# A routed expert layer in pairs of experts: 64 places each, side by side in column halves, with unsplit float32 weights

## The chip, the cores and the metric

The kernel runs on one core of one Trainium2 chip. The metric is the device time of one execution in microseconds (us), the median of several runs. The profile is one further execution, recorded by the hardware profiler; its own time and its span stand below.

## What is computed

The program is one network for 256 tokens of 1024 channels: a first block (three mixing branches, then a routed layer of experts) and a second block of four attention and feed-forward layers. The change is in the routed layer, cut here to what matters:

```python
def hier_moe(h, lp):                       # t: (256, 1024)
    g_logits = t @ lp["moe_rg_w"] + lp["moe_rg_b"]          # 4 groups
    p_top, g_sel = lax.top_k(jax.nn.softmax(g_logits, axis=-1), 1)
    ...                                     # 4 experts in a group, the best two are taken
    e_top, e_sel = lax.top_k(e_in_group, MOE_TOPK)
    w_sel = p_top * jax.nn.softmax(e_top, axis=-1)
    ...
    hg = jnp.einsum("nd,edh->neh", t, lp["moe_w_gate"])      # 16 experts, 1024 -> 256
    hu = jnp.einsum("nd,edh->neh", t, lp["moe_w_up"])
    a = jax.nn.silu(hg) * hu * combine[..., None]
    return jnp.einsum("neh,ehd->nd", a, lp["moe_w_down"])    # 256 -> 1024
```

Each token uses two experts of one group. The result is multiplied by a modulation row and added to the tokens, and a norm and the second block follow. With the inputs of the reference the four groups get 58, 53, 86 and 59 tokens, and no expert gets more than 53.

## The kernel before

Every dense product is a split product: a float32 weight tile is loaded (`raw`, four buffers), ScalarE casts it to a high part (L240), VectorE subtracts to get the low part (L242), and TensorE runs three float32r matmuls, high by high, high by low and low by high (L254, L255, L256). `Core.unit` is that load with its split, `Core.mm3` the three matmuls.

The routed layer is `Block1.moe` (L1451) with its helpers:

- `logits` (L1269) transposes the tokens and multiplies by the routing weights, while `rms` and L1468, L1469 write the normalised tokens `xp` as high and low parts.
- `route` (L1284) is a chain of small VectorE operations in two steps. The first picks each token's group (`top`, L1301 to L1305). `places` (L1337) turns the group marks into places inside the group, by matmuls with a triangle of ones, and reads the fullest group's count into a register of every engine. The second step picks the two experts and their weights.
- `experts` (L1356) works by groups: 128 places a group. One-hot marks (L1370) gather the tokens by matmuls (L1382) into transposed tiles of two groups, which are split again (L1384 to L1386). For each of the 16 experts it streams gate and up weights in four units, 24 matmuls of 512 columns, then SiLU and the product with the token's weight, two transposes (L1444), and the down product of the expert before, 12 matmuls of 512 columns. After each group the result is split and scattered back to the tokens (L1417).
- `add_experts` (L1496) multiplies by the modulation row and adds to the tokens.
- A second, conditional pass for groups of over 128 tokens stands behind it in a block that is skipped at run time (L1493).

TensorE's order is fixed in part by `issue_after`. The eight steps of `mod_row(5)` (L1207), which computes the modulation row from `ada_w`, are the `filler` between `logits`, `route` and `places`. In `ada_steps` (L671, matmul L684) four float32 matmuls stand side by side in 32-column strips. Weight loads go out on SP's queue, small constants and rows on POOL's.

In the second block `enter` (L2026) multiplies the tokens by the final norm's weights (L2037) and transposes them (L370) for the first projection.

## Time and profile before

| | us |
|---|---|
| median of 3 runs | 2035.04 (2033.83 to 2035.51) |
| the profiled execution, its own time | 2037.31 |
| its span in the trace | 2035.5 |
| TensorE busy (PE) | 1931.8 (95%) |
| VectorE busy (DVE) | 1336.6 (66%) |
| ScalarE busy (ACT) | 1035.3 (51%) |
| DMA, mean over the span | 179 GB/s |

PE, DVE, ACT and POOL are the engines' busy times in the span of the profiled execution, which lies 1.8 us under that execution's own time. All places below are us from the start of that span. `arena` is the one large buffer from which most tiles are cut, `mm` and `acc` are PSUM banks (three and five of them), so instructions are told apart by their line. PEld is the loading of weights into the array, and a queue's name ends in q.

### The profile page before, as it was taken

The page shows a single profiled execution, that of the slowest core. Times are in us where ns is not written, and L with a number is a line of the kernel's source. Part 1 is how long each engine was busy: PE and PEld are TensorE (multiplying, and loading weights), DVE is VectorE, ACT ScalarE, POOL GpSimd, SP SyncE. Part 2 cuts the span into 40 slices and gives each one's busy share as a digit, 9 for nine tenths or more (in the row PEclk, how much of TensorE's full clock was granted, in tenths as well). Part 3 has the DMA queues.
Part 4 walks back from the last instruction along what each step waited for, and adds up shares of the span by engine and source line. Part 5 has one row for each costly group of instructions (what it writes and reads, how often), then busy time and mean ns, then how long its engine had stood idle before and what let it go on. Part 6 is the DMA issues. An engine that isn't in the chain of part 4 may idle for free.

```text
span 2035.5 us, 27804 instructions
## 1 busy us (share of the span) xinstructions
PE 1931.8 (95%) x10012; PEld 1546.8 (76%) x10012; DVE 1336.6 (66%) x2324; ACT 1035.3 (51%) x1656; POOL 135.9 (7%) x259
## 2 busy tenths in 40 slices
PE   6998998989998999999999999999999999999997
PEld 2886886867786678887888877887767888767886
DVE  4689887868897775556555466556566555867555
ACT  5555654546774744434655555443563444454442
POOL 2110000000002000002111200000110000300000
PEclk8999998989998899999999999999999999989999
DMA  9546644777995356654543456664554655435662
GB/s 310 162 140 194 183 139 147 236 247 245 321 323 162 116 166 199 186 176 131 170 136 110 147 178 202 191 186 145 156 176 129 201 187 176 155 104 175 188 189 80
DMA packets 272403, 364.61 MB, mean 179 GB/s; under 512 B 17018, under 2 KB 206677, under 8 KB 272256
## 3 DMA queue, kind: packets, MB, share of 16 engines
q1 hardware_dynamic: 264832, 338.38, 52.5%
q0 software_dynamic: 7424, 24.36, 3.8%
q8 instruction: 81, 1.33, 0.3%
q14 instruction: 66, 0.54, 0.1%
HBM read 359.53 MB, written 3.15 MB: 178 GB/s over the span
## 4 chain that ended last, share of the span: by engine, by line
PE 59%; DVE 6%; ACT 2%; DMA 1%; issue 1%; POOL 0%; SPq 0%; DVEq 0%; ACTq 0%; POOLq 0%
PE mm L254 14%; PE mm L255 13%; PE mm L256 13%; PE acc L254 4%; PE acc L256 4%; PE acc L255 4%; PE acc L1752 1%; PE acc L1650 1%; DVE arena L242 1%; PE acc L1929 1%; PE acc L2117 1%; ACT arena L240 1%; DVE arena L2014 1%; PE acc L1749 1%; DMA arena<-in_w_gate_up 1%; PE acc L1925 1%
## 5 line engine op out<-in xcount | busy, mean ns | idle before, releaser
L242 DVE TENSOR_TENSOR arena<-arena,arena 128x1024 fp32r<-128x1024 f32 x597 | 716.9, 1213 | 480.6 <-ACT arena L240 475.8
L240 ACT CAST arena<-arena 128x1024 fp32r<-128x1024 f32 x597 | 614.0, 1039 | 549.4 <-PE mm L256 298.9
L254 PE MATMUL mm<-arena 128*128 128x512 f32 (+1 forms) x1856 | 703.3, 385 | 12.7 <-ACT arena L240 6.8
L255 PE MATMUL mm<-arena 128*128 128x512 f32 (+1 forms) x1856 | 706.0, 381 | 0.3 <-DVE arena L242 0.3
L256 PE MATMUL mm<-arena 128*128 128x512 f32 (+1 forms) x1856 | 698.7, 380 | 3.5 <-DVE arena L1386 1.3
L254 PEld LDWEIGHTS mm<-arena 128*128 128x128 f32 x1856 | 352.9, 191 | 85.8 <-ACT arena L240 8.3
L256 PEld LDWEIGHTS mm<-arena 128*128 128x128 f32 x1856 | 352.3, 191 | 71.2 <-DVE arena L219 4.1
L255 PEld LDWEIGHTS mm<-arena 128*128 128x128 f32 x1856 | 354.0, 191 | 61.5 <-issue 1.8
L254 PE MATMUL acc<-arena 128*128 128x512 f32 (+5 forms) x736 | 235.5, 360 | 7.3 <-ACT arena L218 7.3
L255 PE MATMUL acc<-arena 128*128 128x512 f32 (+5 forms) x736 | 235.4, 351 | 0.5 <-DVE arena L219 0.5
L256 PE MATMUL acc<-arena 128*128 128x512 f32 (+4 forms) x736 | 231.8, 350 | 0.0
L218 ACT CAST arena<-acc 128x512 fp32r<-128x512 f32 (+2 forms) x174 | 92.7, 542 | 179.1 <-PE acc L2117 79.8
L219 DVE TENSOR_TENSOR arena<-acc,arena 128x512 fp32r<-128x512 f32 (+2 forms) x174 | 108.1, 632 | 99.1 <-ACT arena L218 98.7
L254 PEld LDWEIGHTS acc<-arena 128*128 128x128 f32 (+1 forms) x736 | 125.0, 190 | 40.3 <-issue 11.6
L255 PEld LDWEIGHTS acc<-arena 128*128 128x128 f32 (+1 forms) x736 | 125.7, 190 | 21.6 <-issue 1.8
L256 PEld LDWEIGHTS acc<-arena 128*128 128x128 f32 (+1 forms) x736 | 124.7, 190 | 20.5 <-DVE arena L219 1.7
L1685 ACT ACTIVATE arena<-arena,nm 128x128 f32<-128x128 f32 (+2 forms) x128 | 65.9, 517 | 27.1 <-DVE nm L1684 27.1
L768 DVE SCALAR_TENSOR_TENSOR arena<-arena 128x192 f32<-128x192 f32 (+1 forms) x160 | 64.9, 430 | 2.4 <-ACT arena L766 0.9
L1684 DVE CUSTOM_DVE_ANT_0 arena<-acc,arena 128x128 f32<-128x128 f32 (+2 forms) x128 | 53.1, 465 | 13.6 <-PE acc L256 13.6
L370 PE MATMUL acc<-arena 128*128 128x128 f32 x200 | 32.9, 302 | 24.1 <-DVE arena L1020 8.2
L370 PEld LDWEIGHTS acc<-arena 128*128 128x128 f32 x200 | 24.4, 153 | 34.8 <-DVE arena L1020 8.3
L2101 ACT ACTIVATE arena<-mm 128x256 f32<-128x256 f32 x88 | 32.4, 379 | 24.4 <-PE mm L256 11.9
(354 smaller groups left out, 1497.8 us busy)
## 6 DMA issues: line engine op xcount, KB each, us to landing
arena<-in_w_gate_up SPq DMA_DIRECT2D x352, 256.0 KB, 4.0
arena<-in_w_down SPq DMA_DIRECT2D x88, 512.0 KB, 3.6
arena<-in_b_w_qkv SPq DMA_DIRECT2D x144, 256.0 KB, 3.0
arena<-in_w_in SPq DMA_DIRECT2D x56, 512.0 KB, 4.0
arena<-in_ada_w SPq DMA_DIRECT2D x48, 512.0 KB, 5.7
arena<-in_moe_w_gate SPq DMA_DIRECT2D x64, 256.0 KB, 4.6
arena<-in_moe_w_up SPq DMA_DIRECT2D x64, 256.0 KB, 4.9
arena<-in_moe_w_down SPq DMA_DIRECT2D x32, 512.0 KB, 5.3
```

The costliest lines, as they stand in the source:

```text
L218: self.nc.scalar.copy(h, src)
L219: self.nc.vector.tensor_sub(l, src, h.bitcast(F32))
L240: nc.scalar.copy(h[:, : nk * n], raw[:, : nk * n])
L242: nc.vector.tensor_sub(l[:, : nk * n], raw[:, : nk * n], h[:, : nk * n].bitcast(F32))
L254: yield t.matmul(out, x[0], w[0], start=start, stop=False)
L255: yield t.matmul(out, x[0], w[1], start=False, stop=False)
L256: yield t.matmul(out, x[1], w[0], start=False, stop=stop)
L370: self.nc.tensor.transpose(ps[:, j * P : (j + 1) * P], src[:, j * P : (j + 1) * P], self.ident)
L768: nc.vector.scalar_tensor_tensor(ov[:, rows], x, w, ov[:, rows], ALU.mult, ALU.add)
L1684: nc.vector.tensor_tensor_reduce(pr, s, mask, -0.125, 3e38 if sink is None else sink, ALU.add, ALU.min, nm)
L1685: nc.scalar.activation(pr, pr, AF.Exp, bias=nm, scale=-1.0, accum_out=l)
L2101: nc.scalar.activation(s, ps[:, :256], AF.Silu)
```

## The change

- Experts are taken in eight pairs, with 64 places for each expert. The two experts of a pair write partitions 0 to 63 and 64 to 127 of the same PSUM tile, by matmuls on the two column halves of the array.
- The experts' weights and activations are float32 and unsplit: one float32 matmul where three float32r matmuls stood. Loads are 512 KB each with 4 KB in a row, 12 for a pair. To get such rows a partition takes eight consecutive channels; `xp` is written in that order and the two modulation columns are turned into it through DRAM.
- 9216 words of the float32r arena become nine more float32 weight buffers during the layer ("switched"), so that 13 buffers take the loads in turn.
- `route` finds the experts in its first step, and `places` counts places for each expert. The block for experts of over 64 tokens stands after the transposes of the second pair.
- The tokens themselves are put into the sum by a matmul with the identity, each pair's result is multiplied by the modulation row before it is scattered, and the second block reads the sum from PSUM. `add_experts` falls away.
- `mod_row(5)` runs with the Hyena branch, after `mod_row(2)`.

The core of the diff:

```diff
-LATER = (0, 2, 4, 6)
-MORE = (5, 2)
+MORE, SEATS, YP, AMID = 9, 64, 2, 1
-FILL = (3, 4, 1)
...
+    def close_switched(self):
+
+        a = self.arenas[F32R]
...
+        self.arenas["switched"] = Arena(self.switched_room(F32, "f"), SWITCHED)
...
+        turned = []
+        for i, m in enumerate((self.S2, self.A2)):
+            d = self.dram.tile([D], F32, name=f"mod2{i}")
+            nc.gpsimd.dma_start(d.rearrange("(k p) -> p k", p=P), m.rearrange("p k o -> p (k o)"))
+            turned.append(self.tile((KT, 1), F32, f"mod2{i}", 1, "moe"))
+            nc.gpsimd.dma_start(turned[-1].rearrange("p k o -> p (k o)"), d.rearrange("(p k) -> p k", p=P))
...
+        def gather_two(h, g, k):
+            ps = c.mm().rearrange("p (k s) -> p k s", k=2)
+            for j in range(2):
+                cols = slice((k + j) * P, (k + j + 1) * P)
+                for i in range(4):
+                    mm(ps[:, j], xp[i // 2][i % 2][:, cols], marks(i // 2, 4 * g, 4), start=i == 0, stop=i == 3)
+                nc.scalar.activation(h[:, k + j], ps[:, j], AF.Identity, bias=self.S2e[:, k + j], scale=self.A2e[:, k + j])
...
+        def scatter(p, ohT, y):
+            yp = self.parts((D,), "y", YP, "moe")
+            for n in range(2):
...
+                nc.vector.tensor_tensor(f, y[n], self.rows[5][:, sl], ALU.mult)
+                c.split(*(a[:, sl] for a in yp), f)
+            yield
             for t in range(2):
...
+                        mm(acc[t][n], ohT[:, t], yp[i][:, 512 * n : 512 * n + 512], start=False, stop=first == 0 and p == 7 and i == 1)
...
+        for p in range(8):
...
+            hq = [h[:, :, p % 2 * P + 64 * e : p % 2 * P + 64 * e + 64] for e in range(2)]
+            ps = c.acc()
+            for k in range(0, KT, 4):
+                for i, name in enumerate(("moe_w_gate", "moe_w_up")):
+                    us = [load(I[name][0, 2 * p + e].rearrange("(p k) n -> p k n", p=P)[:, k : k + 4]) for e in range(2)]
+                    for j in range(4):
+                        for e in range(2):
+                          with c.after(order):
+                            mm(ps[64 * e : 64 * e + 64, 256 * i : 256 * i + 256], hq[e][:, k + j], us[e][:, j], start=i + k + j == 0, stop=i + k + j == KT)
...
+            with then():
+                next(late, None)
...
+            if p == AMID and amid is not None:
+                with self.tc.If(amid > SEATS):
+                    for n in range(SEATS, 256, SEATS):
+                        self.experts(xp, acc, n, raw)
+                    mark()
+                    for k in range(0, KT // 2, 2):
+                        gather_two(following, 1, k)
+            with then():
+                following = next(later, None)
+            then()
+            y = [c.mm(), c.mm()]
             for kk in range(2):
+                wd = [load(I["moe_w_down"][0, 2 * p + e, kk * P : (kk + 1) * P].rearrange("p (o n) -> p o n", o=1)) for e in range(2)]
+                for n in range(2):
+                    for e in range(2):
+                      with c.after(order):
+                        mm(y[n][64 * e : 64 * e + 64], aT[:, kk, 64 * e : 64 * e + 64], wd[e][:, 0, 512 * n : 512 * n + 512], start=kk == 0, stop=kk == 1)
+            late = scatter(p, ohT, y)
+            next(late)
+            with then():
+                following = next(later, None)
...
+        acc = [[c.acc() for n in range(2)] for t in range(2)]
+        for t in range(2):
+            for n in range(2):
+                with c.after(c.last(PE)):
+                    nc.tensor.matmul(acc[t][n], c.ident, xs[t][:, 512 * n : 512 * n + 512], start=True, stop=False)
...
-        self.add_experts(self.experts(xp, 0, unit), xs)
-        with self.tc.If(most > P):
-            self.add_experts(self.experts(xp, P, own_unit), xs)
+        rooms = rooms()
+        self.experts(xp, acc, 0, lambda: next(rooms), most)
+        return acc
...
-            weave(self.hyena(), self.merge_branch(2, acc), self.mod_row(2))
+            weave(self.hyena(), self.merge_branch(2, acc), chain(self.mod_row(2), self.mod_row(5)))
...
-            for sl in HALVES:
-                nc.vector.tensor_tensor(zs[t][:, sl], xs[t][:, sl], nf[:, sl], ALU.mult)
+            for sl, ps in zip(HALVES, sums[t]):
+                nc.vector.tensor_tensor(zs[t][:, sl], ps, nf[:, sl], ALU.mult)
```

## Rows read from the trace of the kernel before

**Rows 1.** Busy us of each engine by stage, granted clock, DMA share, GB/s.

```profile
355.00:428.00 73.00, 71.87 (x342) 58.40 (x341) 54.44 (x76) 33.73 (x44) 4.47 (x7) 1.00 0.68 223
428.00:459.00 31.00, 23.72 (x172) 17.82 (x172) 24.74 (x76) 13.74 (x25) 1.65 (x3) 0.72 0.83 278
459.00:617.00 158.00, 151.51 (x680) 121.81 (x679) 134.40 (x147) 115.04 (x147) 0.00 (x0) 0.99 0.87 292
```

**Rows 2.** Timeline of TensorE: two experts' beginnings, and the last expert matmul.

```profile
601.74 0.40 PE L254 MATMUL acc<-arena 128*128 128x512 f32 x1
...
610.55 0.40 PE L254 MATMUL acc<-arena 128*128 128x512 f32 x1
...
616.86 0.39 PE L256 MATMUL mm<-arena 128*128 128x512 f32 x1
```

**Rows 3.** Groups of the expert stage, 458.7 to 617: VectorE's weight split.

```profile
L242 DVE TENSOR_TENSOR arena<-arena,arena 128x1024 fp32r<-128x1024 f32 x92 | 110.4, 1223 | 17.5 <-ACT arena L240 15.3 <-DMA arena<-in_moe_w_up 0.6 <-DMA arena<-in_moe_w_down 0.3
```

**Rows 4.** Timeline of TensorE and VectorE: routing, 428 to 459.

```profile
428.15 1.50 PE L684 MATMUL acc<-arena 128*32 128x256 f32 x24
...
439.77 1.27 DVE L1469 SCALAR_TENSOR_TENSOR arena<-arena,rm,arena 128x1024 fp32r<-128x1024 f32 x1
...
443.26 0.15 DVE L1301 TENSOR_REDUCE r<-arena 128x2 f32<-128x8 f32 x1
...
446.81 0.16 DVE L1304 TENSOR_REDUCE r<-arena 128x2 f32<-128x8 f32 x1
447.00 0.17 DVE L1305 TENSOR_TENSOR arena<-arena,r 128x8 f32<-128x8 f32 x1
...
456.03 0.74 PE L1382 MATMUL mm<-arena 128*128 128x256 f32 x4
...
458.73 0.48 PE L254 MATMUL mm<-arena 128*128 128x512 f32 x1
```

**Rows 5.** Line L684 in PSUM `acc`: records, ns min/median/max, places.

```profile
L684 PE MATMUL acc<-arena x128: 379/379/636, 326.0 to 453.0; 128*32 128x256 f32 x128
```

**Rows 6.** Timeline of TensorE: unsplit float32 in four strips, and on the whole array.

```profile
326.05 1.07 PE L684 MATMUL acc<-arena 128*32 128x256 f32 x16
...
339.88 0.64 PE L684 MATMUL acc<-arena 128*32 128x256 f32 x8
340.44 0.39 PE L254 MATMUL acc<-arena 128*128 128x256 f32 x1
...
346.16 1.02 PE L1219 MATMUL acc<-arena 128*128 128x256 f32 x4
```

**Rows 7.** Line L1493, the skipped block: ns of each engine's branch, and place.

```profile
L1493 PEldq COMPARE_BRANCH  x1: 3599/3599/3599, 618.7 to 618.7; - x1
...
L1493 DVEq COMPARE_BRANCH  x1: 72/72/72, 623.3 to 623.3; - x1
L1493 DVEq EVENT_SEMAPHORE  x1: 21/21/21, 626.4 to 626.4; - x1
```

**Rows 8.** A stretch of mixed expert loads, DMA engines full, columns as rows 1.

```profile
509.30:513.30 4.00, 3.69 (x19) 2.73 (x18) 4.00 (x6) 2.79 (x6) 0.00 (x0) 1.00 1.06 394
```

**Rows 9.** DMA packets in 357.3 to 361.3, then in 573.3 to 577.3.

```profile
DMA packets 760, 1.60 MB, mean 401 GB/s; under 512 B 48, under 2 KB 48, under 8 KB 759
...
DMA packets 1437, 1.39 MB, mean 347 GB/s; under 512 B 82, under 2 KB 1437, under 8 KB 1437
```

**Rows 10.** DMA issues on the page: KB each, us to landing.

```profile
arena<-in_w_down SPq DMA_DIRECT2D x88, 512.0 KB, 3.6
```

**Rows 11.** Waits between 320 and 430: us in total, times, longest.

```profile
POOL arena L1260 <- DVE arena L219: 11.9, 1, 11.9
```

**Rows 12.** Timeline of TensorE: the second block's first transposes.

```profile
627.27 1.97 PE L370 MATMUL acc<-arena 128*128 128x128 f32 x8 [7.68 <-DVE arena L2037]
```

**Rows 13.** Stretches with unsplit float32 alone on TensorE, columns as rows 1.

```profile
28.00:36.00 8.00, 5.65 (x53) 2.45 (x52) 6.34 (x24) 7.32 (x15) 2.19 (x4) 1.00 0.98 329
40.00:48.00 8.00, 7.62 (x32) 3.75 (x36) 3.85 (x8) 6.81 (x10) 1.63 (x3) 0.50 0.84 288
```

More of the change, by code (lines that the diff above doesn't have):

```diff
@@ L1321, in route @@
         m2 = top(eg, h2)
+        both = tile(2, 4)
+        v.tensor_tensor(both, h1, h2, ALU.add)
+        spread = lambda x: x.rearrange("p t (o j) -> p t o j", o=1).to_broadcast([P, 2, 4, 4])
+        v.tensor_tensor(self.marks.rearrange("p t (g j) -> p t g j", g=4), spread(both), by, ALU.mult)
+        yield
+        v.tensor_tensor(ex, g, along(mx), ALU.subtract)
+        nc.scalar.activation(ex, ex, AF.Exp)
         q, d = tile(2), tile(2)
@@ L1354, in places, with experts @@
         return nc.values_load(most_i[0:1, 0:1], min_val=0, max_val=256)
-    def experts(self, xp, first, unit):
+    def experts(self, xp, acc, first, raw, amid=None):
         c, nc, I = self.c, self.nc, self.I
         tile = lambda shape, dt, tag, bufs=1: self.tile(shape, dt, tag, bufs, "moe")
-        parts = lambda shape, tag, bufs=1: self.parts(shape, tag, bufs, "moe")
+        mm = nc.tensor.matmul
         pos = self.pos
         if first:
-            pos = tile((2, 4), F32, "later")
+            pos = tile((2, 16), F32, "later")
@@ new lines, in experts, with then @@
+        late, later = iter(()), iter(())
+        order = c.last(PE)
+        def then():
+            nonlocal order
+            order = c.last(PE)
+            return c.after(order)
+        for p in range(8):
+            if p % 2 == 0 and p:
+                h = following
+            if p % 2 == 0 and p < 6:
+                later = gather(p // 2 + 1)
+            hq = [h[:, :, p % 2 * P + 64 * e : p % 2 * P + 64 * e + 64] for e in range(2)]
[7 more added lines that the diff above has]
+                            mm(ps[64 * e : 64 * e + 64, 256 * i : 256 * i + 256], hq[e][:, k + j], us[e][:, j], start=i + k + j == 0, stop=i + k + j == KT)
+            wp = c.mm()[:, :2]
+            for t in range(2):
+                mm(wp, marks(t, 2 * p, 2).bitcast(F32), self.comb[:, t, 2 * p : 2 * p + 2], start=t == 0, stop=t == 1)
+            for e in range(2):
+                rows = slice(64 * e, 64 * e + 64)
+                nc.scalar.copy(weight[rows, p : p + 1], wp[rows, e : e + 1])
@@ L1445, in experts @@
-            aT = parts((2, P), "aT", 2)
-            c.split(*(x.rearrange("p k t -> p (k t)") for x in aT), ps[:, : 2 * P])
-            pend = (e, aT, y)
-        down(*pend)
-        return acc
-    def moe(self, xs, fill):
-        c, nc = self.c, self.nc
-        def filler(n):
-            for _ in range(n):
-                with c.after(c.last(PE)):
-                    next(fill)
-        filler(FILL[0])
+            nc.vector.scalar_tensor_tensor(a, ps[:, 256:], weight[:, p : p + 1], s, ALU.mult, ALU.mult)
@@ L1460, in moe @@
+            next(late)
+            with then():
+                following = next(later, None)
+            then()
+        next(late)
+    def moe(self, xs):
+        c, nc = self.c, self.nc
+        c.close_switched()
         pss = self.logits(xs)
         first = c.last(DVE), c.last(ACT)
-        filler(FILL[1])
         r = self.rms(xs, [c.norm_f_tile()] * 2)
@@ L1496, in add_experts, with rooms @@
-    def add_experts(self, acc, xs):
-        for t in range(2):
-            for n in range(2):
-                sl = slice(512 * n, 512 * n + 512)
-                a = self.tile((512,), F32, "moa", 2, "moe")
-                self.nc.vector.tensor_tensor(a, acc[t][n], self.rows[5][:, sl], ALU.mult)
-                self.nc.vector.tensor_tensor(xs[t][:, sl], xs[t][:, sl], a, ALU.add)
+        other = lambda: c.arenas["switched"].ring("moe", "wx", 1024, MORE)
+        def rooms():
+            while True:
+                for f, n in ((c.raw, RAW), (other, MORE)):
+                    for _ in range(n):
+                        yield f()
@@ L1571, in run @@
                 self.dump(f"mix{t}", xs[t])
-            self.moe(xs, self.mod_row(5))
-            for t in range(2):
-                self.dump(f"moe{t}", xs[t])
+            sums = self.moe(xs)
             drop("moe", "mrow5")
-        return xs
+        return xs, sums
 def rope_tables(c):
@@ L2163, in network @@
         b1 = Block1(core)
-        xs = b1.run()
+        xs, sums = b1.run()
         core.first_block_done()
-        Block2(core, b1.tables).run(xs, out)
+        Block2(core, b1.tables).run(xs, sums, out)
 def kernel(**inputs):
```

184 lines of the change are left out of this document (83 added, 101 removed).

## The prediction, made before the changed kernel was run

> **What bounds it now.** I read the busy times by stage first. From 459 to 617 the routed experts keep TensorE busy 151.5 of 158 us at a granted clock of 0.99, while VectorE has 134 and the DMA engines a share of 0.87 [rows 1]. So TensorE sets the pace, and the timeline gives it: one expert every 8.81 us, for 36 matmuls of 512 columns and two transposes, or some 0.23 us a matmul [rows 2]. VectorE's weight split, 110 us of 92 subtractions [rows 3], lies beside that. Ahead of it, from 428 to 459, TensorE's clock is 0.72 on average [rows 1] and the path is VectorE's chain of small routing operations, broken by weight splits: the normalised tokens end at 441.04, the next routing operation starts at 443.26, and its fourth only at 446.81, though two dependent ones need 0.19 us each [rows 4]. Behind it the last expert matmul starts at 616.86 [rows 2] and the second block's first transposes at 627.27 [rows 12]: between them lie the scatter, eight VectorE operations and the skipped block, where TensorE's branch alone takes 3.6 us [rows 7].
>
> **Ahead of the experts.** `mod_row(5)` moves to a stage in which TensorE is busy 71.9 of 73 us [rows 1], so its work is paid there. Half of the 128 records of L684 in `acc` are its own: 64 records for 32 matmuls, so an unsplit float32 matmul runs as two passes [rows 5]. In four strips 16 passes take 1.07 us, and full-width passes come every 0.214 us, (1.02 - 0.379)/3 [rows 5, 6]; a change between strips and full width costs 0.13 us, since eight passes, worth 0.43, hold the next matmul up by 0.56 [rows 6]. That makes 16 rounds of 0.215, eight passes of L1219 and some sixteen changes: 3.4 + 1.7 + 1.7 = 6.8 us. I take all of it; the end for a stage that hides half is 3.4. Its four more megabytes of loads lie beside a DMA share of 0.68 [rows 1].
>
> In the routing stage the path loses the first filler passes (1.4 of the 1.50 in [rows 4]), the 2.2 us between 441.04 and 443.26, 2.9 of the 3.6 us that three operations took up to 446.81, and one split of 1.2 ahead of 439.77 [rows 3, 4]. It gains 15 small operations at 0.2 for the experts' choice ahead of `places`, 3.0. The one-hot marks cost about the same (two operations of 1.2 for 2.2 us). From the first gather matmul to 458.73 only the 32 matmuls at about 0.15 [rows 4] remain: I count 3.1 less, because the weights, the low parts and the filler no longer stand between. Together -7.8; I take -6.5, for a cold clock. Reading `xp` with a stride costs nothing, or at most the same again for two operations of 1.27 [rows 4], 2.5 us. The identity matmuls, 8 passes of 512 columns, 3.4 us or 6.8 at half clock, lie in TensorE's wait for VectorE, from which the whole chain above is cut; if that wait is gone they are paid. On POOL's queue the two turns through DRAM stand ahead of the routing weights; L1260, which uses them, waits 11.9 us for VectorE now [rows 11], and four transfers in two dependent steps at some 4 us each, as in [rows 10], fit under that. **Sum: +6.8 - 6.5 = +0.3.** The experts begin some 30.9 us after the mixing ends instead of 30.6, all told.
>
> **The experts on TensorE.** Per pair: 32 gate and up matmuls are 64 passes of 256 columns, two at a time on the column halves: 32 x 0.215 = 6.9. Down: 8 rounds of 512 columns, 3.4. Scatter: 8 x 0.23 = 1.8. Weights and four transposes 0.9 (two transposes leave 0.5 of the 8.81). Six changes between halves and full width at 0.13, 0.8. That is 13.8 us, where two experts took 17.6 [rows 2, 6]. Gathers for the next pairs, 96 matmuls in six pairs at 0.14, add 13 us. Total 8 x 13.8 + 13 = 123, and the skipped block's branch of 3.6 in the middle [rows 7] with a few short hand-overs makes about **131**, where 158.5 stood (458.73 to 617.2).
>
> **The experts on the DMA queue.** The skipped block names all 13 weight buffers, so every load that follows it in SP's order has to wait until TensorE has left it: now ScalarE and VectorE wait for one another there in the same way [rows 7]. Ahead of it stand pair 0's 12 loads and pair 1's gate and up, 20 in all; 76 of 524,288 bytes follow. TensorE comes to the block after about 13.8 + 2.2 + 10 = 26 us, loses 3.6, and finds nothing loaded. From there the loads pace it. Packets of at least 2 KB moved at 401 GB/s, those of at most 1 KB at 347 [rows 9], a mixture at 394 [rows 8]. I take 400, as 4 KB rows are nearest to the first: 1.31 us a load. A load lands 3.6 us after its issue [rows 10], 2.3 more than that. 26 + 3.6 + 2.3 + 76 x 1.31 + 1.7 for the last half of the down product = **133**. The two sums are so close that they disturb each other; I add 3 and take 136. **-22.5.** The ends: 123 + 3.6 if both are kinder (-32), and 26 + 7.6 + 76 x 1.39 + 3 = 142 at 377 GB/s, the middle of the two rates (-16).
>
> The page DMA: Bandwidth & Descriptors of the Trainium skill gives (Specifications) about 358 GB/s as the HBM limit of one core; the trace has 394 and 401 over 4 us, so the measurement decides. By the page's figure a load would take 1.46 us, and the forecast would be 12 us later.
>
> **Behind the experts.** From the last down matmul to the first transposes I count: multiply, split, split and five scatter matmuls 4.2, a norm product 0.7, hand-overs 0.4: 5.3 instead of 10.4 (616.86 to 627.27). `add_experts` and the branch fall away. The sums hold four of the five `acc` banks, so the second four transposes wait for the first to be copied; I count 0.3 of this stage's gain as lost to it. **-4.8**, between -3 and -8. VectorE and ScalarE lose 96 splits, but those lay beside TensorE: nothing for them by themselves.
>
> **Sum.** 0.3 - 22.5 - 4.8 = -27.0. The profiled execution took 2037.31, 2.3 above the median of 2035.04 [the table above]. 2037.3 - 27.0 = 2010.3, and against the median **2008.0**. The case's own range, with the ends given: 1997 to 2017.
>
> **Rivals.**
> *The loads come at the lower rate.* If 4 KB rows keep only the 347 GB/s of the small packets [rows 9], a load takes 1.51 us and 76 of them 15 us more: 2023. For it: half of this queue's traffic before was of that kind and the stage's own mean is 292 [rows 1]; against it: the rate rose with the packets. This is also the outcome under the page's limit above, some 3 us earlier. Chance 0.15.
>
> *The two halves run one after the other.* Then each pair pays 6.9 + 3.4 us more, TensorE's sum rises from 131 by 82 to 213, and the time is 2008 + 77 = 2085: slower. The place is the gate, up and down matmuls of each pair; it decides from the point where a second half costs 0.4 of a pass of its own, since 131 + 0.4 x 82 = 164 eats the whole gain. Against it speak the four strips, which take one full-width pass together [rows 6]; for it, that no row has two 64-column halves with different moving data of this length. Chance 0.05.
>
> *The clock falls while TensorE waits for loads.* From 40 to 48 unsplit float32 kept TensorE busy 7.6 of 8 us and the granted clock was still 0.50, the 1.2 GHz level; from 28 to 36 it was 1.00 with 5.65 of 8 us [rows 13]. If the stretch behind the block ran at 1.2 GHz, its 97 us of TensorE work (six pairs, the end of the second and four pairs' gathers) would be 194 in place of 106: 2008 + 88 = 2096. Against it: in that stretch TensorE would be busy nine tenths of the time, with all rows of the array. Chance 0.06. The Trainium skill's page TensorE: Matmul & The Clock Gate (HAM oscillation) describes such a fall where each tile's work is shorter than the wait for its load; in the expert stage before, with its short waits, the clock is 0.99 [rows 1].
>
> *The change does not do what it says* would be the block being entered. The fullest expert has 53 of 64 places, so I give that nothing.
>
> **How the numbers follow.** The main case gets 0.66, the rivals 0.15, 0.05 and 0.06. The 0.08 left is for what I have no row for, such as a buffer of the switched room that comes free late: 0.05 for a gain between 5 and 25 us, 0.03 for within 0.2% (4 us, about what a measurement of this kernel can tell from no change). Faster: 0.66 + 0.15 + 0.05 = 0.86; same 0.03; slower 0.05 + 0.06 = 0.11. The range has to hold 0.8: nearly all of the main case and most of the slow-load one, 1996 to 2025.
>
> **What would show it.** In the changed profile: pairs of 256-column passes every 0.215 us in two halves; no float32r cast of expert weights; a gap on TensorE of about 3.6 us and then waits for `moe_w_down` in the second pair, with DMA near idle just before it; then a DMA share near 1 and about 400 GB/s to the end; about 136 us from the first gate matmul to the last down matmul; some 5 us from there to the second block's transposes; and L684 in the Hyena stage. It would be wrong if loads were issued across the block, if the stretch behind it were paced by TensorE, or if the routing chain did not get shorter.

## The result, and the profile after

The changed kernel is slower: 2060.93 us (median of 4 runs, 2055.21 to 2063.74) against 2034.43 (4 runs, 2031.33 to 2035.51) for the kernel before, a ratio of 1.0132, 95% interval 1.0115 to 1.0148. The forecast was 2008. The profiled execution of the changed kernel took 2055.21 us with a span of 2053.4, so the two traces compared here are 17.9 us apart. The other 8.6 of the 26.5 us between the medians are spread between executions: the profiled one of the kernel before took 2.9 us more than its median, that of the changed kernel was the fastest of its four.

Places that both kernels pass tell where the time went. Two groups of the trace of before give its logits and its feed-forward transposes (ns min/median/max, first and last start in us):

```profile
L1281 PE MATMUL acc<-arena x32: 266/266/382, 432.0 to 436.7; 128*128 128x40 f32 x32
L2117 PE MATMUL acc<-arena x176: 270/272/275, 742.6 to 2015.4; 128*128 128x128 f32 x176
```

The same lines of the changed kernel, with the down matmuls between them (L1521, unsplit):

```profile
L1317 PE MATMUL acc<-arena x32: 266/266/383, 455.3 to 460.2; 128*128 128x40 f32 x32
L1521 PE MATMUL mm<-switched_f,arena x124: 592/592/1116, 489.9 to 632.7; 128*64 128x512 f32 x124
L2181 PE MATMUL acc<-arena x176: 270/272/275, 753.3 to 2033.3; 128*128 128x128 f32 x176
```

| TensorE, us | before | after | stretch, after less before |
|---|---|---|---|
| first logits matmul | 432.0 | 455.3 | +23.3 |
| first gate matmul | 458.7 | 479.5 | -2.5 |
| last expert matmul starts | 616.9 | 632.7 | -5.0 |
| first feed-forward transposes | 742.6 | 753.3 | -5.1 |
| last feed-forward transposes | 2015.4 | 2033.3 | +7.2 |

The experts are only 5 us shorter, and two stretches that the forecast held to be almost or quite untouched are longer by 23 and 7 us.

**Ahead of the logits.** Two stretches of the changed kernel, columns as [rows 1]:

```profile
360.00:400.00 40.00, 30.40 (x195) 21.03 (x189) 22.85 (x42) 11.55 (x21) 3.23 (x6) 0.91 0.67 222
400.00:451.00 51.00, 51.00 (x238) 42.27 (x237) 34.48 (x40) 22.37 (x27) 0.00 (x0) 1.00 0.60 196
```

Before, TensorE was busy all 40 us from 360 to 400, at full clock:

```profile
360.00:400.00 40.00, 40.00 (x200) 33.91 (x199) 34.00 (x52) 19.93 (x27) 4.47 (x7) 1.00 0.70 230
```

Now it has 30.40, and its waits from 380 to 400 (us in total, times, longest) begin with `mod_row(5)`'s own sums, L1248 behind ScalarE's copy L719:

```profile
PE acc L1248 <- ACT arena L719: 3.6, 1, 3.6
PE mm L285 <- ACT arena L271: 2.3, 1, 2.3
```

Further ahead POOL's two trips through DRAM stand, between 195 and 245 and not beside the routing. POOL's wait for them, then the DMA packets from 205 to 235:

```profile
POOL arena L1286 <- DMA mod<-arena: 20.4, 2, 10.9
```

```profile
DMA packets 8633, 5.18 MB, mean 173 GB/s; under 512 B 239, under 2 KB 8077, under 8 KB 8632
```

**Routing**, answering to [rows 4]: the logits, the identity matmuls, the first count in `places`, the gathers and the first gate matmuls on the timeline.

```profile
455.32 5.23 PE L1317 MATMUL acc<-arena 128*128 128x40 f32 x32
460.38 5.52 PE L1552 MATMUL acc<-arena 128*128 128x512 f32 x8
469.23 0.40 PE L1384 MATMUL mm<-arena 128*128 128x16 f32 x2 [3.32 <-DVE arena L1359]
...
471.73 6.41 PE L1427 MATMUL mm<-arena 128*128 128x256 f32 x28 [1.21 <-DVE arena L1417]
...
479.45 3.67 PE L1482 MATMUL acc<-arena 128*64 128x256 f32 x32
```

The first 28 gathers take 0.23 us each instead of 0.15, at a granted clock of 0.59 from 470 to 475. VectorE's two operations that write the low parts of `xp` now read the tokens with a stride; the first of them on the timeline (1.27 in [rows 4]):

```profile
460.71 2.09 DVE L1545 SCALAR_TENSOR_TENSOR arena<-arena,rm,arena 128x1024 fp32r<-128x1024 f32 x1 [1.32 <-ACT arena L1544]
```

**Experts**, answering to [rows 2, 7]: the end of the second pair's transposes, the block, and one later pair.

```profile
504.34 0.38 PE L1500 MATMUL mm<-arena 128*128 128x128 f32 x2
508.63 1.20 PE L1427 MATMUL mm<-arena 128*128 128x256 f32 x4 [3.91 <-PEq L1506]
...
512.66 7.27 PE L1521 MATMUL mm<-switched_f,arena 128*64 128x512 f32 x16 [0.90 <-DMA switched_f<-in_moe_w_down]
...
566.62 0.73 PE L1457 MATMUL acc<-arena 128*128 128x512 f32 x2
567.28 1.73 PE L1482 MATMUL acc<-arena 128*64 128x256 f32 x13
569.16 1.19 PE L1457 MATMUL acc<-arena 128*128 128x512 f32 x4
570.40 1.94 PE L1482 MATMUL acc<-switched_f,arena 128*64 128x256 f32 x14
573.39 0.44 PE L1500 MATMUL mm<-arena 128*128 128x128 f32 x2 [0.80 <-DVE arena L1492]
```

Three things cost here. The block holds TensorE for 3.9 us; the down product behind it takes 7.27 us where others take 3.65, at the 1.2 GHz level (granted clock 0.50 from 510 to 515); and in the later pairs scatter matmuls (L1457) stand in the middle of the next pair's gate and up matmuls (L1482), after which TensorE waits for VectorE's product L1492. Pairs 2 to 5, counted from 0, take 18.8 to 21.0 us from one start to the next. Loads hardly hold TensorE up: of its waits from 478 to 634 (us in total, times, longest) one is for a load.

```profile
PE mm L1500 <- DVE arena L1492: 6.6, 7, 1.1
...
PE mm L1521 <- DMA switched_f<-in_moe_w_down: 0.9, 1, 0.9
```

The DMA packets from 496 to 510 show the queue idle ahead of the block and in it:

```profile
DMA packets 27, 0.16 MB, mean 11 GB/s; under 512 B 0, under 2 KB 0, under 8 KB 21
```

**Behind the experts**, answering to [rows 12]: the first transposes start 6.1 us after the last down matmul instead of 10.4, but four and four. The third group stood 8.8 us behind the first (636.08, the first in [rows 12]); now it stands 11.4 behind it.

```profile
636.08 1.03 PE L370 MATMUL acc<-arena 128*128 128x128 f32 x8
```

```profile
638.77 0.66 PE L401 MATMUL acc<-arena 128*128 128x128 f32 x4 [1.01 <-DVE arena L2101]
...
643.43 0.65 PE L401 MATMUL acc<-arena 128*128 128x128 f32 x4 [1.19 <-DVE arena L250]
...
650.13 0.60 PE L401 MATMUL acc<-arena 128*128 128x128 f32 x4
```

**The second block.** 160 us of one feed-forward layer, columns as [rows 1], before and then after:

```profile
745.00:905.00 160.00, 160.00 (x725) 132.24 (x724) 84.76 (x90) 72.64 (x89) 0.00 (x0) 1.00 0.65 201
```

```profile
757.00:917.00 160.00, 160.00 (x715) 130.22 (x714) 82.56 (x87) 71.55 (x87) 0.00 (x0) 1.00 0.62 197
```

TensorE is busy without a gap at full clock in both, and yet gets through 715 matmuls instead of 725. The instructions are the same. From first to last transposes a feed-forward layer takes 168.0 to 168.3 us instead of 165.7, four times.

### The profile page after: what moved, and what is told of

It is laid out like the page before. It is cut to its first block, busy times and chain, and to the rows that moved or that the text cites. A ratio compares the mean times of both kernels' runs of the same rounds, so it can differ in the third digit from the quotient of the medians.

```text
span 2053.4 us, 27705 instructions
## 1 busy us (share of the span) xinstructions
PE 1929.3 (94%) x10188; PEld 1502.6 (73%) x10188; DVE 1216.0 (59%) x2192; ACT 950.9 (46%) x1587; POOL 138.3 (7%) x263
## 4 chain that ended last, share of the span: by engine, by line
PE 64%; DVE 6%; ACT 2%; DMA 2%; issue 1%; POOL 0%; SPq 0%; DVEq 0%; ACTq 0%; POOLq 0%
PE mm L285 13%; PE mm L286 13%; PE mm L287 13%; PE acc L285 4%; PE acc L287 4%; PE acc L286 4%; PE acc L1482 2%; PE mm L1521 1%; PE acc L2181 1%; PE acc L1993 1%; PE acc L1714 1%; PE acc L1816 1%; DVE arena L2078 1%; ACT arena L271 1%; DMA arena<-in_w_gate_up 1%
## 5 line engine op out<-in xcount | busy, mean ns | idle before, releaser
L271 ACT CAST arena<-arena 128x1024 fp32r<-128x1024 f32 (+1 forms) x449 | 461.2, 1034 | 491.3 <-PE mm L287 245.0
L285 PE MATMUL mm<-arena 128*128 128x512 f32 (+1 forms) x1458 | 547.0, 382 | 18.7 <-ACT arena L271 12.0
L287 PE MATMUL mm<-arena 128*128 128x512 f32 (+1 forms) x1490 | 557.6, 377 | 1.5 <-DVE arena L764 1.5
L273 DVE TENSOR_TENSOR arena<-arena,arena 128x1024 fp32r<-128x1024 f32 (+1 forms) x302 | 361.0, 1200 | 312.3 <-ACT arena L271 310.3
L286 PE MATMUL mm<-arena 128*128 128x512 f32 (+1 forms) x930 | 341.9, 368 | 0.7 <-DVE arena L273 0.7
L285 PEld LDWEIGHTS mm<-arena 128*128 128x128 f32 x1458 | 278.6, 192 | 77.3 <-ACT arena L271 15.0
L287 PEld LDWEIGHTS mm<-arena 128*128 128x128 f32 x1490 | 284.9, 192 | 55.7 <-DVE arena L250 2.3
L286 PE MATMUL mm<-switched_r,arena 128*128 128x512 f32 x718 | 286.0, 398 | 0.0
L273 DVE TENSOR_TENSOR switched_r<-arena,arena 128x1024 fp32r<-128x1024 f32 x147 | 179.7, 1223 | 139.9 <-ACT arena L271 139.7
L286 PEld LDWEIGHTS mm<-arena 128*128 128x128 f32 x930 | 180.6, 194 | 27.7 <-issue 1.6
L285 PE MATMUL acc<-arena 128*128 128x512 f32 (+3 forms) x532 | 179.7, 369 | 5.2 <-ACT arena L249 5.1
L286 PEld LDWEIGHTS mm<-switched_r,arena 128*128 128x128 f32 x718 | 135.1, 188 | 28.7
L287 PE MATMUL acc<-arena 128*128 128x512 f32 (+1 forms) x404 | 155.3, 389 | 0.0
L286 PE MATMUL acc<-arena 128*128 128x512 f32 (+1 forms) x392 | 150.6, 386 | 0.0
L285 PEld LDWEIGHTS acc<-arena 128*128 128x128 f32 (+1 forms) x532 | 91.2, 188 | 31.6 <-issue 8.1
L285 PE MATMUL mm<-switched_r,arena 128*128 128x512 f32 x190 | 75.9, 400 | 0.1
```

What stands on the lines that cost most here:

```text
L271: nc.scalar.copy(h[:, : nk * n], raw[:, : nk * n])
L273: nc.vector.tensor_sub(l[:, : nk * n], raw[:, : nk * n], h[:, : nk * n].bitcast(F32))
L285: yield t.matmul(out, x[0], w[0], start=start, stop=False)
L286: yield t.matmul(out, x[0], w[1], start=False, stop=False)
L287: yield t.matmul(out, x[1], w[0], start=False, stop=stop)
```

## The experiments

"Logits" is the start of the first logits matmul, "experts" the time from the first gate matmul to the start of the last down matmul, both from the trace.

### Four parts undone or done alone

**a_mod5_fill**: the row computed in the routing stage again.

```diff
-            weave(self.hyena(), self.merge_branch(2, acc), chain(self.mod_row(2), self.mod_row(5)))
+            weave(self.hyena(), self.merge_branch(2, acc), self.mod_row(2))
...
-            sums = self.moe(xs)
+            sums = self.moe(xs, self.mod_row(5))
```

> The changed kernel with mod_row(5) alone put back where it was before (three steps ahead of logits, four behind, one behind places). Theory: the stretch up to logits is 23 us later in the changed kernel (432.0 to 455.3) because mod_row(5)'s steps outlast the Hyena branch and then stand alone, waiting for their loads and for each other; undone, logits begin at about 435 and the routing gives back some 4 us: 2041 to 2049 us. Rival 1: the stretch is longer for the two turns through DRAM, which hold the weight loads up around 205 to 235, or for the split room: then logits stay behind 448 and the time is 2055 to 2064. Rival 2: only the 7 us of its own work count: 2052 to 2056.

2034.16 us, ratio to before 1.0003 (0.9989 to 1.0016). Logits at 440.0 instead of 455.3, and from there to the first gate matmul 25.1 us instead of 24.2. The move costs 15 us where it was put and saves 1 where it was taken from. The time lies below all three ranges, and logits are 5 us later than the theory had them, so only the place of the loss is as the theory says.

**a_no_turn**: no trips through DRAM.

```diff
-            d = self.dram.tile([D], F32, name=f"mod2{i}")
-            nc.gpsimd.dma_start(d.rearrange("(k p) -> p k", p=P), m.rearrange("p k o -> p (k o)"))
...
+        self.S2e, self.A2e = self.S2, self.A2
```

> The changed kernel without the two turns of the modulation columns through DRAM; the columns are used unturned, so this part of the computation is left out. Theory: the turns fill the DMA queues for two stretches of some 10 us (205 to 213 and 227 to 237, under 60 GB/s), and 3 of the 3.5 us by which the kernel is late at 320 us are theirs: 2056 to 2059 us. Rival 1: what they hold up is hidden, since the VectorE chain of the mLSTM branch ends later anyway: 2059.5 to 2062.5. Rival 2: they delay the Hyena stage's loads for good and with that make up most of the 23 us ahead of logits: 2040 to 2050.

2041.43 us, 1.0036 (1.0021 to 1.0051); logits at 445.5, 9.8 us earlier. Neither the theory's 3 us nor "hidden": the trips count, which is nearest to the second rival (5 more of the 19.5 us that the total gained lie in the experts, 147.9, whose order changed with it). The packets from 205 to 235, against the 8633 above:

```profile
DMA packets 12074, 7.00 MB, mean 233 GB/s; under 512 B 224, under 2 KB 11488, under 8 KB 12072
```

**b_room**: the kernel before, its float32r arena in two tiles.

```diff
+SWITCHED = 9216
...
+            if dt == F32R:
+                words -= SWITCHED
...
+        return self.ap[:, at : at + n] if at < self.words else self.switched[:, at - self.words : at - self.words + n]
```

> The kernel before, with nothing changed but that 9216 words of the float32r arena lie in a tile of their own (nothing is switched). Theory: the gate and up matmuls of the second block's feed-forward layers come every 233 ns instead of 227 because their low parts lie in that room; 4 layers of some 480 such matmuls, 6 ns each: 11 us at most, 7 taken: 2038 to 2046 us, and a pitch near 233 ns in the trace. Rival: the pitch has another cause (the order of the loads, the clock): 2031 to 2037 and a pitch of 227 ns.

2037.81 us, 1.0009 (0.9997 to 1.0022). The feed-forward layers take 167.8 to 168.3 us, as in the changed kernel, 9 us in all; ahead of the first of them the kernel is 6.3 us earlier (logits at 428.4), which hides most of it in the total and puts that just under the theory's range.

**a_no_block**: the conditional block left out.

```diff
-        self.experts(xp, acc, 0, lambda: next(rooms), most)
+        self.experts(xp, acc, 0, lambda: next(rooms))
```

> The changed kernel without the conditional block for experts of over 64 places (left out). Theory: TensorE loses there 3.9 us at the block, 0.9 us for the first load behind it, and 3.6 us because the down product behind it runs at half the clock, some 3 us more in the pair after it: 9 to 11 us, 2050 to 2053. Rival 1: the loads pace the stage all along, so that a queue that starts 12 us earlier brings it all back: 2043 to 2049. Rival 2: it is only the 3.9 us: 2056 to 2058.

2036.37 us, 1.0002 (0.9988 to 1.0016). The experts take 131.3 us instead of 153.2: 22 us, more than any of the three expectations. A pair takes 16.7. Logits moved by +4 to 459.5 without any edit there. That is not another order of the work: TensorE's 2378 instructions ahead of the logits stand in the same order in the changed kernel, here, and in a_own, a_pe_only, a_dma_only and a_late below, and logits begin between 455.1 and 459.7 in the six traces. Here the 4 us arise between 389 and 402, at a lower clock. The stretch from 396 to 404 in the changed kernel and then here:

```profile
396.00:404.00 8.00, 8.00 (x37) 6.45 (x36) 5.88 (x8) 4.43 (x5) 0.45 (x1) 1.00 0.91 307
```

```profile
396.00:404.00 8.00, 8.00 (x25) 6.51 (x26) 4.78 (x8) 3.54 (x5) 0.45 (x1) 0.65 0.78 246
```

So 4 us at the logits, read from one execution each, are no proof of an edit's cost.

### What the block costs, and who sets the pace

**a_own**: the block uses the four buffers loaded last before it.

```diff
                 with self.tc.If(amid > SEATS):
+                    spare = cycle(used[-4:])
                     for n in range(SEATS, 256, SEATS):
-                        self.experts(xp, acc, n, raw)
+                        self.experts(xp, acc, n, lambda: next(spare))
```

> The changed kernel with the conditional block kept where it is, but its loads go to the four buffers that were loaded last before it, in place of all 13, so that the next nine loads need not wait for it. In the changed kernel the experts take 153.2 us from the first gate matmul to the start of the last down matmul, without the block 131.3. Theory: of these 22 us most is the queue that stands idle from 496 to 511 us, in a stage that the loads pace at some 350 to 400 GB/s; with it running on, 134 to 140 us remain (3.9 at the block, a slow clock behind it): 2040 to 2048. Rival 1: SP itself cannot pass the block before TensorE, so the idle stretch stays: 150 to 154 us and 2055 to 2064. Rival 2: the loss is TensorE's clock behind the block: 145 to 150 us.

2040.99 us, 1.0055 (1.0029 to 1.0081); experts 139.2, a pair 16.7 again. That fits the theory's number, but its reason was not yet shown, for TensorE's order changed as well: in this build, as without the block, no scatter stands inside a pair's gate and up matmuls up to pair 6. TensorE's time at the block:

```profile
512.46 1.19 PE L1427 MATMUL mm<-arena 128*128 128x256 f32 x4 [5.48 <-PEq L1506]
```

**a_pe_only**: no block, and the first pair's twelve loads used for all pairs.

```diff
+            if first == 0 and len(kept) == 12:
+                kept.append(kept.pop(0))
+                return kept[-1].rearrange("p (k n) -> p k n", k=src.shape[1])
```

> The changed kernel without the conditional block and without 84 of its 96 expert weight loads: the twelve of the first pair are used for every pair, so the computation is that of other weights. The stage then has TensorE's own length. It is 131.3 us without the block alone. Theory: the loads and TensorE are so nearly equal there that TensorE alone takes 126 to 130 us. Rival 1: TensorE alone sets the 131.3 and nothing changes within 1 us. Rival 2: the loads set it, at 1.31 us each, and TensorE alone takes 118 to 125.

2043.57 us (one run); experts 136.9, which none of the three expected: 3.9 of it are a new wait ahead of the last down product, and that product takes 6.6 us instead of 3.7. A pair takes 16.7 as without the block (up to pair 4; one more 17.5). So TensorE sets the 16.7 by itself, the first rival's mechanism if not its number.

**a_dma_only**: no block, three of four gate and up matmuls left out, all loads kept.

```diff
-                    for j in range(4):
+                    for j in range(1):
```

> The changed kernel without the conditional block, with three of every four gate and up matmuls left out (only the first of the four slices of each load is used); all 96 loads stay. TensorE then has some 11.5 us of work a pair in place of 16.7, so the loads set the pace. In the changed kernel 76 loads behind the block took 115.1 us, 1.51 each. Theory: the queue keeps only about 350 GB/s over 100 us, whatever TensorE does, though it reaches 420 over 10 us: 1.45 to 1.53 us a load. Rival: the queue alone keeps 395 to 420 GB/s, 1.25 to 1.33 us a load, and the 1.51 came from buffers that TensorE gave back late.

2009.96 us (one run). The rival: 83 loads in 110.0 us, 1.325 each. The stretch, columns as [rows 1]:

```profile
481.00:590.00 109.00, 92.27 (x438) 47.58 (x440) 22.45 (x40) 29.98 (x76) 3.22 (x6) 0.96 1.02 413
```

413 GB/s over 109 us. The queue is no slower over a long time than in the 4 us of [rows 8, 9], so the 1.51 us a load of the changed kernel is not its own rate. It is TensorE's pace: from pair 4 on the loads were issued within about 1 us of the last matmul that used their buffer.

**a_late**: the block as it was, but the scatter held behind the last gate and up matmul.

```diff
+            gu = c.last(PE)
             wp = c.mm()[:, :2]
...
-            with then():
+            with c.after(gu):
                 next(late, None)
```

> The changed kernel with one edit: the scatter matmuls of a pair are held until the last gate and up matmul of the next pair has been issued. Its conditional block still names all 13 buffers. In the changed kernel the scatters and mark transposes stand in the middle of the gate and up matmuls of pairs 2 to 7, those 64 passes take 8.9 to 10.3 us in place of 6.7, and TensorE then waits some 1 us for the product; without the block, and with its own buffers, they stand behind them and a pair takes 16.7 us. Theory: behind the block it is this order, not the loads, that makes a pair 18.8 to 21.0 us; held back, a pair takes 16.7 to 17.5, the experts 139 to 144 us from first gate to last down matmul, and the kernel 2045 to 2052. Rival: the loads pace those pairs, as the forecast had it with 1.51 us a load; then the scatters leave the gate and up matmuls waiting: 150 to 154 us, 2056 to 2062.

2052.11 us, 1.0104 (1.0076 to 1.0131); experts 143.7, pairs 3 to 5 17.2 each. The theory's numbers, at the upper edge in the total, with logits 4.4 us later in this execution. A later pair on the timeline:

```profile
565.13 3.62 PE L1482 MATMUL acc<-arena 128*64 128x256 f32 x32
568.58 1.90 PE L1482 MATMUL acc<-switched_f,arena 128*64 128x256 f32 x16
570.41 2.12 PE L1457 MATMUL acc<-arena 128*128 128x512 f32 x8
572.36 0.38 PE L1499 MATMUL mm<-arena,arena 128*128 128x128 f32 x2
572.58 0.38 PE L1501 MATMUL mm<-arena 128*128 128x128 f32 x2
```

The scatter now fills the wait for the product. a_no_turn and a_turn, whose block is the changed kernel's, show the same inside one execution: pairs with all eight scatters inside the gate and up matmuls take 19.4 to 19.6 us (2 and 3), the next two, with one or two inside, 16.7 and 17.5. So of the 22 us of the block, 9.5 are the order (153.2 - 143.7); 4.5 more lie between that and a_own (139.2), where the loads flow on; and 7.9 are the block itself (139.2 - 131.3): 5.5 us on TensorE's queue there, and the gathers and the down product behind it at the lower clock (4.9 us instead of 3.7).

### The two tiles

**b_room_pad, b_room_3328, b_room_3584**: b_room with the second tile 32, 96 and 160 words further on.

```diff
-SWITCHED = 9216
+SWITCHED, PAD = 9216, 32
...
-.tile([P, SWITCHED], dt, name=f"switched_{name}")
+.tile([P, PAD + SWITCHED], dt, name=f"switched_{name}")[:, PAD:]
```

> The kernel before with 9216 words of the float32r arena in a tile of their own, as in the run with the room alone, but that tile begins 32 words further on, so that its words lie 3072 bytes behind where they lay in one arena instead of 2944 (3072 is a multiple of 1024). In the run with the room alone each feed-forward layer took 168.3 us from its first to its last transposes instead of 165.7. Theory: the slower pitch comes from the place of the low parts relative to the high parts, and a round offset takes it away: 165.5 to 166.2 us a layer, 227 ns, and some 10 us less in all, near 2028. Rival 1: it comes from a second tile as such, or from an offset that must be rounder still: 168 us a layer, 2035 to 2040.

> The kernel before with the room in a tile of its own, beginning 96 words further on: 3328 bytes behind its old place, which is 13 x 256. At 2944 bytes (23 x 128) a feed-forward layer took 168.0 us from the first to the last of its transposes, at 3072 (12 x 256, 3 x 1024) 165.6. If a multiple of 256 bytes is enough: 165.6; if it must be a multiple of 512 or of 1024: 167 to 169.

> The same with the room 160 words further on: 3584 bytes behind its old place, which is 7 x 512. If a multiple of 512 bytes is enough: 165.6 us a layer; if it must be a multiple of 1024: 167 to 169.

2026.75 us, 0.9975 (0.9963 to 0.9988), then 2027.98 and 2024.41 (one run each). In all three a layer takes 165.6 to 165.7 us. 160 us of a layer in b_room_pad, columns as [rows 1]; b_room has 715 matmuls in the same window:

```profile
740.00:900.00 160.00, 160.00 (x726) 132.20 (x726) 84.94 (x90) 72.21 (x89) 0.00 (x0) 1.00 0.65 202
```

The second tile as such costs nothing; its offset does. No trace shows an address: the 2944 bytes are worked out from the kernel's allocations, and only the steps of 128, 384 and 640 bytes from it are the edits' own.

### The trips, the row, and the repaired kernel

**a_turn**: the columns transposed on TensorE ahead of the trip.

```diff
-            nc.gpsimd.dma_start(d.rearrange("(k p) -> p k", p=P), m.rearrange("p k o -> p (k o)"))
+            ps = c.tr()[:KT, :P]
+            nc.tensor.transpose(ps, m.rearrange("p k o -> p (k o)"), c.ident)
...
+            nc.scalar.copy(rows, ps)
+            nc.gpsimd.dma_start(d.rearrange("(k p) -> k p", p=P), rows)
```

> The changed kernel with one repair: the two modulation columns are turned by a TensorE transpose, so that each trip through DRAM is written as eight rows of 512 bytes instead of 1024 single values of 4 bytes. Without the trips at all logits began at 445.5 us instead of 455.3 and the time was 2041.4. Theory: it is the write by single values that holds up the weight loads (their 512-byte packets took 1 to 5 us each between 205 and 236); so logits begin at 444 to 448 and the time is 2038 to 2046. Rival: any trip through DRAM at this place costs as much, the read back in rows of 32 bytes above all: logits at 452 to 457, 2054 to 2063.

2043.20 us, 1.0063 (1.0040 to 1.0085); logits at 449.6, between the two cases. The traces settle the other 4.1 us. At 382 us a_turn is 0.8 us behind a_no_turn, and some 11 ahead of the changed kernel; the rest is lost between 384 and 392, where TensorE is busy 4.8 of 8 us at a granted clock of 0.80, in a_no_turn 6.8 at 1.00. So it is the write by single values that costs, the read back next to nothing, and idle time with a lower clock at the end of the stage takes a part of the gain again.

**b_mod5**: the kernel before with only `mod_row(5)` moved.

```diff
-            weave(self.hyena(), self.merge_branch(2, acc), self.mod_row(2))
+            weave(self.hyena(), self.merge_branch(2, acc), chain(self.mod_row(2), self.mod_row(5)))
...
-            self.moe(xs, self.mod_row(5))
+            self.moe(xs, iter([None] * 8))
```

> The kernel before with nothing changed but mod_row(5), which follows mod_row(2) beside the Hyena branch as in the changed kernel (the routing stage has no filler). Theory: its last steps outlast the Hyena branch and stand alone, so logits begin 12 to 18 us later (444 to 450), and the routing gives back 1 to 4 us: 2042 to 2052. Rival 1: only its own work counts, 6.8 us, less what the routing gains: 2034 to 2040. Rival 2: the move costs only together with the trips through DRAM or the second tile, and nothing here: 2030 to 2036.

2056.38 us, 1.0100 (1.0070 to 1.0129): this move alone loses most of what the whole change loses. Logits at 457.5, 25.5 us later, more than the theory's 18; 2.0 of them stand already at 362, ahead of the moved work. The routing gives 3.2 back. TensorE from 360 to 400, where it was busy throughout before:

```profile
360.00:400.00 40.00, 28.78 (x161) 20.88 (x161) 20.91 (x38) 9.11 (x17) 3.23 (x6) 0.79 0.66 215
```

11.2 us without work and a clock of 0.79 come on top of the row's own 6.8.

**best1**: the changed kernel with a_mod5_fill, a_turn, a_own and the 32 words.

> The changed kernel with four repairs: mod_row(5) in the routing stage as before; the block with four buffers of its own; the modulation columns turned on TensorE first, so that the trip through DRAM is written in eight rows of 512 bytes instead of 1024 single values; the room 32 words further on. Theory: logits begin near 432 us (before 432.0), the routing takes 25, the experts 137, 15 more to the second block's transposes, so they begin some 27 us earlier than before, and the second block costs 0 (room repaired) to 10 us (not repaired) more: 2006 to 2020. Rival: the repairs give the same time back twice and the order of the work moves elsewhere: 2022 to 2036.

2006.66 us (4 runs) against 2031.60, a ratio of 0.9884 (0.9861 to 0.9906): faster than both kernels. Logits at 429.1, experts 135.8, a layer 165.7. This is the change's gain with these four costs repaired.

**best1b0**: the same, with `mod_row(5)` beside the last merge branch.

```diff
-            weave(self.merge_branch(0, acc))
+            weave(self.merge_branch(0, acc), self.mod_row(5))
```

> The repaired kernel (block with its own four buffers, columns turned on TensorE, room 32 words on) with mod_row(5) not in the routing stage but beside the last merge branch, ahead of it. Theory: mod_row(5) as work in a stage where TensorE is always busy costs its own 6.8 us, and of the 15.3 us that the changed kernel lost by it the other 8.5 were waits of steps that stood alone: logits at 434 to 437 instead of 429.1, and the routing 0 to 1 us shorter: 2011 to 2016. Rival 1: its work costs nothing there, as the steps fall into short waits: 2005 to 2008. Rival 2: it costs the full 15 also there: 2019 to 2024.

2020.78 us, 0.9945 (0.9926 to 0.9963); logits 18 us later, the second rival's numbers; from the logits to the first gate matmul 24.2 us instead of 27.3. It is inconclusive on the theory, since a wait of another kind came in, the ones matmul of the routing weights (us in total, times, longest):

```profile
PE acc L1304 <- POOL arena L1299: 8.2, 1, 8.2
```

## Why the prediction was wrong, point by point

**Ahead of the experts, forecast +0.3, measured +20.8.** This step failed. `mod_row(5)` was priced as 6.8 us of TensorE work in a stage that was busy 71.9 of 73 us. But it is more than that work: each half is a chain of loads, strips, a ScalarE copy and sums, and where it stands alone TensorE waits for that chain. Alone in the kernel before it cost 25.5 us, undone in the changed one it gave 15.3 back. With the 9.8 of the trips below, the 15.3 make 25.1, enough for the 23.3 by which logits are late. Why the move costs more in the kernel before stays open; executions with the same order of work differ by up to 4 us at this place. The sum has a slip as well, of 0.4 us: sixteen changes at 0.13 are 2.1, not 1.7. A stage that shows no idle time has no room for a chain, and "half hidden" to "fully paid" did not bound it from above.

The two trips through DRAM were costed at nothing, with POOL's wait of [rows 11] as cover. They cost 9.8 us, for two reasons that no row of before showed: the build put them at 205 to 235, and what they took was not POOL's time but that of the DMA queues, where 40 of the 7838 packets of 512 bytes took 1 to 5.1 us (median 29 ns), against none in a_no_turn and a_turn.

The routing chain got shorter by 2.5 us, not 6.5. The gathers were priced at 0.15 us as in [rows 4] and ran at 0.23, most of them at the 1.2 GHz level after TensorE's wait for VectorE, 2.2 us in all. Reading `xp` with a stride was put at nothing, with 2.5 us as the bound: VectorE's two operations took 2.08 us each instead of 1.27, and ScalarE's two ahead of them 2.2 instead of 1.1. The identity matmuls took 5.5 us, but hidden, as forecast: TensorE still waited 3.3 us for VectorE behind them.

**The experts, forecast 136, measured 153.2.** The pieces were nearly right. TensorE came to the block after 25 us (26), lost 3.9 (3.6), the loads behind it did wait, and without the block the stage took 131.3 (131 less 3.6, so 4 us were missing from the sum). The queue's 1.31 us a load was right too, 1.325 alone. What failed is the step that took the larger of two nearly equal sums and added 3. The two do not just run side by side: the order of TensorE's matmuls is laid down when the kernel is built, and with the loads held back behind the block it was laid down with scatters inside the gate and up matmuls. That order then cost 9.5 us, though the loads came in time (0.9 us of waiting for one). And the block was priced at its branch of 3.6 us; with the gathers and the product behind it at a lower clock it is 7.9. The end of the range took 377 GB/s as the middle of 401 and 347, which is 374: 0.8 us.

The rival of the lower load rate named the right time, 1.51 us a load and 151 us, for a wrong reason: a_dma_only shows the queue at 413 GB/s. The page DMA: Bandwidth & Descriptors of the Trainium skill has two figures for this, some 358 GB/s as one core's limit (Specifications) and 425 GB/s measured on a single core over 16 MB (Bandwidth); here 413 GB/s is nearer the second.

The two column halves did run at the same time: 64 passes of 256 columns in 6.9 us, as forecast, and 16.0 us a pair with gathers became 16.7. The clock did fall, as the third rival said, but for three products (7.3, 5.4 and 5.1 us instead of 3.7) and not for the stretch, where it is 0.94 on average from 479 to 633.

**Behind the experts, forecast -4.8.** The first transposes came 4.3 us sooner, and the split into four and four, counted at 0.3, gave 2.5 of it back (from the first to the third group 11.4 us, where 8.8 stood). The mechanism was right, one term too small.

**The second block was not in the sum at all.** That 9216 words of the float32r arena become weight buffers was read as a matter of the experts alone. The room stays a tile of its own to the end of the kernel, and 10 us of feed-forward work came from its offset.

**What held.** With the four side costs repaired the kernel is at 2006.7 us, where 2008.0 was forecast for the change: experts 135.8 (136), logits to first gate 27.3. But it is another kernel, and its sum has other terms: a feed-forward layer takes 165.7 us again, and the row is back in the routing stage, where it costs 1.0 us by a_mod5_fill and some 3 by b_mod5 and best1b0. So the agreement of the two totals is in part luck.

## What to carry to other kernels

Moving work into a fully busy stage costs its waits as well as its work: price the chain (load, copy, sum), not the matmuls, and keep it where another wait covers it. Before costing a small rearrangement through DRAM at nothing, ask what its single-value packets do to the queues that the weights use, and when the build will really issue it. When a buffer pool is cut in two, compare a stage far from the edit that reads from both parts, and where two sums come out equal, do not add a margin but ask which order of the work hides the last wait.

## What the runs showed of the hardware

- **Where the operands lie changes TensorE's pitch.** Where matmuls of 512 columns read now from one tile and now from another (high and low parts of weights), they came every 234 to 236 ns (medians) instead of 227, without a wait or a change of clock, when the second tile lay 2944 bytes (23 x 128) behind its place in one arena; at 3072, 3328 and 3584 (12, 13 and 14 x 256) it was 226 to 227 again. Four offsets in all, worked out from the allocations, so a rule "multiples of 256" is what they agree with, not more; the cause is open.
- **Writes of single 4-byte values hold up other queues.** For 1024 of them POOL waited up to 10.9 us, and 40 of the 7838 packets of 512 bytes beside them, from 205 to 235, took 1 to 5.1 us (median 29 ns). Written as eight rows of 512 bytes (a_turn) none took over 0.42.
- **Loads in 4 KB rows kept 413 GB/s for 109 us** on one core, with buffers free in time (a_dma_only).
- **A skipped block costs more than its branch.** TensorE lost 3.9 (changed kernel) and 5.5 us (a_own) in it, and a_own took 7.9 us more than without the block, with what follows it at a lower clock.
- **A strided read costs on VectorE and ScalarE.** Operations on 128x1024 that read in steps of eight words took 2.08 and 2.2 us instead of 1.27 and 1.1.
